# A list-scheduled hybrid decoder layer: two kinds of PSUM tiles change banks, and the schedule's transfer rate changes

## The chip, the cores and the metric

The kernel runs on one core of one Trainium2 chip. The metric is the device time of one execution in microseconds (us), taken as the median of several runs. Lower is better.

A core has a TensorE for matrix products (PE in the profile, with its weight loads as PEld), VectorE (DVE), ScalarE (ACT), GpSimd (POOL) and SyncE (SP). Here SP issues nearly all DMA transfers. TensorE writes its results to PSUM, which has eight banks; VectorE and ScalarE read them from there.

## The reference: what is computed

One layer over 4096 tokens of width 1024. The input is normalised, modulated with a scale and a shift from a conditioning vector, and projected once. The projection feeds three groups of heads in parallel:

- sliding-window attention (window 128, eight query heads, two key/value heads, with sinks and a distance penalty),
- RWKV-7 time mixing (four heads, a recurrent state with data-dependent decay and a delta rule),
- gated linear attention, GLA (four heads, in chunks).

```
h = rmsnorm(x, g_pre) * (1 + scale) + shift
proj = h @ w_in
attn = sliding_window_attention(q, k, v, sinks) * silu(ag)
rwkv = rwkv7_mixer(h, r, k, v, ...) * silu(rg)      # S = S*w + sa (kk*a) + v k ; y = S r
gla  = gla_mixer(h, q, k, v, ...) * silu(gg)
y = concat([attn, rwkv, gla]) @ w_out
out = x + gate * rmsnorm(y, g_post)
```

The change touches how two intermediate results of the RWKV part are held: the running sums of the log decay, from which the decay factors of a chunk come, and the transposed keys, which update the recurrent state.

## The kernel before

The tokens are cut into 16 steps of 256 (`NS`, `NT`). The kernel has two phases over these steps.

**First phase (about the first 1000 us).** For each step i a set of stages runs, each a Python generator:

- `stage_a` (line 1014) loads the tokens, normalises them and writes `hT`, the split f16 input of the projections; it uses PSUM tile `rb`.
- `stage_p` projects: tiles `pv`, `lp`, `zz` and `gqk`, all in bank pair `pj`. These are long runs of f16 products.
- `stage_d` (called "w") makes the gates and decays: `zp`, `gp`, `cgp`, then `wps` and `aps`, then the two tiles `cw`. A `cw` tile holds running sums of the log decay for one of the two 64-token chunks of each half step: a matmul of the decays `gw` with a constant triangular table. ScalarE reads each `cw` tile twice and writes `ep` and `em`, the exponentials of plus and minus the sums.
- `stage_qa`, `stage_qb` and `stage_qc` build and invert the triangular system inside a chunk: `np`, `atp`, then a pass through DRAM, then `Xp`, `Xq`, `Xp`, `X2`.
- `stage_k` (line 1470) transposes the keys: twice per step four 128x128 transposes go to a tile `kp`, and ScalarE copies it in three pieces to `BK`, of which there is one buffer.
- `stage_v` (`vp`, `bp`) and `stage_r` (`ktp`, `gap`, `kvp`, `op`, `ot`) do the values and the GLA part.
- `stage_q2` (line 1486) runs the recurrence over four chunks: `rp`, `up`, `sp`, `yp`, and at its end transposes the output in a tile `yt`.
- `stage_c` and `stage_g` convert the weights of the second phase on the side.

**Second phase.** `stage_s` does the projections for attention and the attention, `stage_m` mixes the three groups, and `outp` does the output projection with seven products per step (`op`), whose weights partly come in anew (`ov<-woscr`), and the last norm.

**PSUM.** The function `pst(tag, name)` (line 477) takes a 2 KB tile in the bank named by its tag. The tags are `pj` (two buffers), `m`, `mq`, `tr`, `at`, `sq` and `y`. With one buffer a tile can be written only when all reads of the tile before it under that tag are over, and tiles of a tag follow one another in the order in which the program asked for them. In the first phase `mq` serves `ktp`, one of the two `gap`, `kvp`, `ot`, `vp`, one of `np`, `bp` and `atp`, `Xp`, `Xq`, `X2`, `kp` and `yt`; `tr` serves `rb`, `aps` and one `cw`; `m` serves `zp`, `gp`, `cgp`, `wps` and the other `cw`; `at` serves `op` and the other `gap`, `np`, `bp` and `atp`.

**What sets the order.** Two planners act one after the other. `emit` (line 549) interleaves the stages: at each turn it takes the first stage, by rank, that can go on by a rough clock. A stage says with its `yield` what it waits for, tiles or bank names; `stage_k` names `mq` and `stage_d` names `m` and `tr`. So the order of the program comes about, and with it the order of tiles in each bank. Then `Order.pin` (line 222) makes a list schedule of every instruction of a phase: it keeps a ready time for each, takes the ready one with the lowest rank (its place in the program, with offsets for some), and fixes the order on each engine by dependencies. For a transfer it uses a table of landing times by size (3.5 us up to 512 KB, 4.8 us above) and a pipe shared by all transfers: a transfer lands no sooner than the pipe's time, which is at least 1.7 us after its issue and moves on by the bytes over a rate. `pin` is called for the first phase at line 1567 and for the second at line 2038. Transfers at the start of the second phase (its first weights) stand before that second list.

Of the kernel before, what the change touches and what calls it, by code (L numbers as in the profile page):

```python
# [33 lines left out]
LIFT = {}  # L34
LAG = {"l": 150}
URGENT = 150
TILING_WAIT = 0.6
LANES = ((0.06, 1.04e-3, VL), (0.02, 1.0e-3, AL), (0.1, 2.3e-3, 0.0), (0.0, 1e-3 / 2.4, PL), (0.05, 0.0, 2.0))

# [24 lines left out]
class Order:  # L64
# [157 lines left out]
    def pin(self):  # L222

        steps = self.steps
        ready = {e: {} for e in ENGINES}
        bursts, head = {}, list(range(len(steps)))
        for k, st in enumerate(steps):
            if st.eng == "PE":
                h = head[k - 1] if k else 0
                if k and steps[h].eng == "PE" and st.joint and st.joint == steps[h].joint and st.array[0] == steps[h].array[0]:  # L230
                    head[k] = h
                bursts.setdefault(head[k], []).append(k)
        left, when = [0] * len(steps), [0.0] * len(steps)
        for k, st in enumerate(steps):
            for j in [*st.needs, *st.turn]:
                if head[j] != head[k]:
                    left[head[k]] += 1
                    steps[j].then.append(k)
        for k, st in enumerate(steps):
            if head[k] == k and not left[k]:  # L240
                ready[st.eng][k] = 0.0
        free = dict.fromkeys(ENGINES, 0.0)
        cells, mode, table, pipe, half = [0.0] * 16, None, None, 0.0, {}
        last, count = {}, 0
        while count < len(steps):
            e = min((e for e in ENGINES if ready[e]), key=lambda e: max(free[e], min(ready[e].values())))
            now = max(free[e], min(ready[e].values())) + 1e-9
            at = sorted((k for k, t in ready[e].items() if t <= now), key=lambda k: (steps[k].rank, k))
            k = at[0]
            if e == "PE" and mode is not None and steps[k].array[0] != mode:  # L250

                same = [q for q in at if steps[q].array[0] == mode]
                wait = max(now - ready[e][q] for q in at if steps[q].array[0] != mode)
                if same and (mode != (4, 4) or wait < TILING_WAIT):
                    k = same[0]
            first = max(free[e], ready[e].pop(k))
            for k in bursts.get(k, [k]):
                st, t = steps[k], max(first, free[e])
                if e == "PE":
                    m, at, passes, took, issue = st.array  # L260
                    if mode is not None and m != mode:
                        t = max(t, max(cells)) + 0.094
                    mode = m
                    t = max(t, max(cells[c] for c in at))
                    for c in at:
                        cells[c] = t + passes * took
                    free[e], st.end = t + issue * passes, t + passes * took + 0.165
                else:
                    if st.half is not None:
                        was, half[e] = half.get(e, st.half), st.half  # L270
                        if was[0] != st.half[0] or None not in (was[1], st.half[1]) and was[1] != st.half[1]:
                            t = max(t, free[e] + 0.115)
                    if st.table is not None and st.table != table:
                        t, table = max(t, free[e] + 1.28), st.table
                    free[e], st.end = t + st.occ, t + st.lat
                    if st.bytes:

                        pipe = max(pipe, t + 1.7) + st.bytes / 310e3
                        st.end = max(st.end, pipe)
                st.start = t  # L280
                if e in last:
                    self.tc.add_manual_dep(
                        st.ins, last[e], mybir.DependencyInfo(mybir.DependencyClass.NoSync, mybir.DependencyReason.DATA))
                last[e], count = st.ins.name, count + 1
                for q in st.then:
                    to, h = steps[q], head[q]
                    left[h] -= 1
                    at = t if k in to.turn else 0.0
                    if k in to.needs and e != to.eng:
                        at = max(at, st.end + HOP_FROM[e] + HOP_INTO.get(to.eng, 0.0))  # L290
                    elif k in to.needs and (e == "SP" or e != "PE" and to.needs[k]):
                        at = max(at, st.end + (0.05 if e == "SP" else 0.03))
                    when[h] = max(when[h], at)
                    if not left[h]:
                        ready[to.eng][h] = when[h]
        self.forget()
# [104 lines left out]
def hybrid_kernel(ctx, tc, x, xc, rows, ada1, adaw, w1, wl, w2, wo, cst, abias, out):  # L401
# [8 lines left out]
    def pool_of(at, name, bufs=1, **kw):  # L410
        return model.order.pool(at.enter_context(tc.tile_pool(name=name, bufs=bufs, **kw)), bufs)
# [4 lines left out]
    st = pool_of(ctx, "small", 3)  # L416
# [57 lines left out]

    ps = pool_of(ctx, "ps", 1, space=PSUM)

    def pst(tag, name, bufs=1):
        bufs = 2 if tag == "pj" else bufs
        t = ps.tile([P, 512], F32, tag=tag, name=name, bufs=bufs)
        model.take(tag, bufs, t.tensor.name)  # L480
        return t
# [31 lines left out]
    def proj(po, W, c0, cw, hT):  # L513

        whi, wlo = W[0], W[1]
        n = 0
        for k in range(KD):
            for a, b in ((whi, 0), (whi, 1), (wlo, 0)):
                PE.matmul(po, a[:, k, c0 : c0 + cw], hT[:, b, k, :], start=(n == 0), stop=(n == 3 * KD - 1))
                n += 1  # L520
            yield
# [27 lines left out]
    def emit():  # L549

        while live:
            live.sort(key=lambda s: s[:2])
            best = None
            for s in live:
                if any(k[1] >= 0 and k not in done for k in s[4]):
                    continue
                t = max([s[5]] + [model.bank(b) for b in s[6]])
                if best is None or t < when:
                    best, when = s, t
                if t <= PE.clock:  # L560
                    break
            assert best is not None, [(s[2], s[1], s[4]) for s in live]
            PE.clock = max(PE.clock, when)
            model.now = PE.clock
            model.lift, model.stage, model.at = LIFT.get(best[2], 0), best[2], best[1]
            need = next(best[3], done)
            if need is done:
                done.add((best[2], best[1]))
                live.remove(best)
                continue  # L570
            need = () if need is None else need if isinstance(need, list) else [need]
            best[4] = [k for k in need if isinstance(k, tuple)]
            best[5] = max([PE.clock if not need else 0.0] + [model.time(t) for t in need if isinstance(t, bass.AP)])
            best[6] = [k for k in need if isinstance(k, str)]
# [65 lines left out]
    with ExitStack() as p1:  # L640
# [924 lines left out]
                    (8, "a", stage_a, i), (9, "c", stage_c, i), (10, "p", stage_p, i))  # L1565
        emit()
        model.order.pin()


    def pool2(name):  # L1570
# [78 lines left out]
    def heads_of(hT, q, kT, vt_, pj, pv):  # L1649
# [4 lines left out]
        yield from proj(kp[:, :NT], Wq[2], 0, P, hT)  # L1654
        model.order.urgent = URGENT
        for kv in range(2):
# [7 lines left out]
        for n in range(2):  # L1664
            yield ["pj"]
            qp = pj("qp")
            for b in range(2):
                yield from proj(qp[:, b * NT : (b + 1) * NT], Wq[n], b * P, P, hT)
            model.order.urgent = URGENT
            for kv in range(2):  # L1670
# [7 lines left out]
        for a in range(2):  # L1678
            yield from proj_tok(vp[:, a * P : (a + 1) * P], Wq[2], P, P, hT, a * P)
        model.order.urgent = URGENT  # L1680
        S.activation(vt_.rearrange("p a n -> p (a n)"), vp[:, :NT], AF.Identity, scale=Wq[2][2])
# [16 lines left out]
    def gates_of(hT, ag, pj):  # L1698

        for n in range(4):  # L1700
# [4 lines left out]
            av = ag[:, 2 * n : 2 * n + 2, :].rearrange("p b n -> p (b n)")  # L1705
            model.order.urgent = URGENT
            S.activation(av, gp_, AF.Tanh, scale=g_h[n])
# [182 lines left out]
    def outp(i):  # L1890
# [31 lines left out]
        def full(n):  # L1922
            yield ["pj"]
            po = pjt("op")
            yield from product(po, n)
            f["po"] = po

        def add(to, z):
            model.order.urgent = URGENT
            V.tensor_tensor(to, f["po"], z, op=ALU.add)  # L1930
            model.order.urgent = 0
# [9 lines left out]
        for y, n in first:  # L1941
            yield from full(n)
            model.order.urgent = URGENT
            S.copy(y, f["po"])
# [290 lines left out]
```

## Time and profile before

The median of three runs is 2021.44 us, from 2020.94 to 2027.34. The profiled execution took 2023.94 us; its span, from the first to the last instruction, is 2022.1 us.

| Engine | busy us | share of the span | instructions |
|---|---|---|---|
| TensorE | 1919.5 | 95% | 24899 |
| TensorE weight loads | 1483.7 | 73% | 24899 |
| VectorE | 1506.7 | 75% | 4246 |
| ScalarE | 1130.1 | 56% | 2609 |
| GpSimd | 311.3 | 15% | 485 |

The transfers move 258.77 MB, a mean of 128 GB/s. The mean granted clock of TensorE is 0.989.

How to read it: busy time is the union of an engine's instructions. Matmuls are pipelined, so their durations overlap, and a busy TensorE is not one at its peak. In the rows, `out<-in` names the tile written and the tiles read, with buffer numbers left out; `xN` counts instructions, and the bracket gives the idle time of the engine before the first one and what ended it. Nearly all instructions are recorded by one helper and therefore carry the same line, 336; tiles tell them apart. Some matmul records can be missing from a trace.

### The profile page before, as it was taken

What the parts mean: (1) busy time and instruction counts of PE and PEld (TensorE: products, weight loads), DVE (VectorE), ACT (ScalarE), POOL (GpSimd) and SP (SyncE); (2) the same over time, 40 slices, a digit from 0 to 9 for tenths busy, and PEclk for the clock granted to TensorE, in tenths of its full rate; (3) what the DMA queues carried; (4) which work ended last, traced back from release to release, by engine and by line L of the source; (5) the groups of instructions that cost most, each with busy time, mean ns of one, the idle gap of its engine ahead of it and who ended that gap; (6) DMA issues with size and microseconds to landing.
All of it is one profiled execution on the core that took longest, in us unless ns stands there. A gap on an engine that the chain in (4) does not pass through costs nothing.

```text
span 2022.1 us, 59931 instructions
## 1 busy us (share of the span) xinstructions
PE 1919.5 (95%) x24899; PEld 1483.7 (73%) x24899; DVE 1506.7 (75%) x4246; ACT 1130.1 (56%) x2609; POOL 311.3 (15%) x485
## 2 busy tenths in 40 slices
PE   5899999999999999999989999999999999999997
PEld 1677787777787777877767678877778777787683
DVE  5777877887778887776758876777767777676866
ACT  5878778765866765555434544444454444444443
POOL 0622213262221222221100000000000000000001
PEclk8899999999999999999999999999999999999998
DMA  9464535353424411124243433344333443334414
GB/s 373 150 208 148 164 114 160 118 150 110 131 76 147 151 37 60 61 76 141 93 152 125 154 106 117 117 139 139 97 108 116 149 129 112 110 108 141 128 36 168
DMA packets 154267, 258.77 MB, mean 128 GB/s; under 512 B 49026, under 2 KB 100738, under 8 KB 147716
## 3 DMA queue, kind: packets, MB, share of 16 engines
q1 hardware_dynamic: 153844, 254.34, 38.8%
q8 instruction: 198, 3.24, 0.6%
q14 instruction: 81, 0.66, 0.1%
q10 hardware_dynamic: 144, 0.52, 0.1%
HBM read 193.98 MB, written 60.82 MB: 126 GB/s over the span
## 4 chain that ended last, share of the span: by engine, by line
PE 54%; DVE 22%; ACT 9%; DMA 8%; issue 4%; SPq 2%; POOL 1%; DVEq 0%; ACTq 0%; POOLq 0%
PE gp L336 16%; PE op L336 12%; PE zz L336 4%; PE qp L336 3%; PE pv L336 2%; PE lp L336 2%; PE kp L336 2%; PE sc L336 2%; DVE pr L336 2%; PE ovp L336 2%; DVE q L336 2%; DVE mtp L336 2%; SPq L336 2%; DMA cs<-in_wo 1%; DVE tsc L336 1%
## 5 line engine op out<-in xcount | busy, mean ns | idle before, releaser
L336 PEld LDWEIGHTS <-mtp 128*128 128x128 f16 x1344 | 130.7, 98 | 146.0 <-issue 6.3
L336 PE MATMUL op<-o,mtp 128*128 128x512 f16 x768 | 172.9, 380 | 0.0
L336 ACT ACTIVATE pr<-pr,nm,lsc 128x256 f32<-128x256 f32 (+1 forms) x256 | 149.0, 584 | 11.5 <-DVE nm L336 11.4
L336 PE MATMUL op<-ov,mtp 128*128 128x512 f16 x576 | 144.0, 381 | 3.6 <-DMA ov<-woscr 3.5
L336 PEld LDWEIGHTS <-hT 128*128 128x128 f16 x1536 | 120.5, 100 | 24.5 <-issue 3.9
L336 ACT ACTIVATE mtp<-yv,oi 128x1024 f16<-128x1024 f32 x30 | 34.5, 1149 | 155.1 <-DVE yv L336 114.4
L336 DVE CUSTOM_DVE_ANT_0 pr<-sc,ab,kept 128x256 f32<-128x256 f32 (+1 forms) x256 | 108.4, 475 | 15.5 <-PE sc L336 15.2
L336 POOL TENSOR_TENSOR ry<-sy,expo 128x1 f32<-128x1 f32 x30 | 19.1, 638 | 588.3 <-DVE sy L336 588.3
L336 PE MATMUL pv<-gvh,hT 128*128 128x272 f16 x512 | 101.0, 290 | 5.6 <-ACT hT L336 2.6
L336 DVE TENSOR_TENSOR yv<-op,yv 128x512 f32<-128x512 f32 x105 | 70.3, 681 | 47.3 <-PE op L336 33.4
L336 DVE SCALAR_TENSOR_TENSOR ag<-ag,gp 128x512 f32<-128x512 f32 x64 | 43.4, 678 | 67.8 <-ACT ag L336 67.7
L336 PE MATMUL zz<-hT,rh 128*128 128x256 f16 x512 | 91.8, 277 | 1.7 <-DVE x L336 1.7
L336 PE MATMUL lp<-hT,Lh 128*128 128x256 f16 x512 | 91.3, 274 | 1.7 <-issue 1.6
L336 PE MATMUL zz<-hT,kh 128*128 128x256 f16 x512 | 91.9, 273 | 0.0
L336 ACT ACTIVATE ag<-gp,gh 128x512 f32<-128x512 f32 x64 | 43.9, 686 | 83.3 <-PE gp L336 83.3
L336 PE MATMUL qp<-hT,q1h 128*128 128x256 f16 x512 | 86.3, 273 | 3.7 <-DVE kT L336 3.7
L336 PE MATMUL zz<-hT,vh 128*128 128x256 f16 x512 | 89.4, 275 | 0.0
L336 PE MATMUL gqk<-hT,gqkh 128*128 128x256 f16 x512 | 87.5, 273 | 1.1 <-DVE zb L336 1.1
L336 PE MATMUL gp<-hT,q5h 128*128 128x256 f16 x512 | 86.3, 273 | 0.0
L336 PE MATMUL qp<-hT,q0h 128*128 128x256 f16 x512 | 85.4, 273 | 0.0
L336 PE MATMUL gp<-hT,q3h 128*128 128x256 f16 x512 | 85.3, 273 | 0.0
L336 PE MATMUL gp<-hT,q6h 128*128 128x256 f16 x512 | 85.2, 273 | 0.0
(442 smaller groups left out, 5858.5 us busy)
## 6 DMA issues: line engine op xcount, KB each, us to landing
ov<-woscr SPq DMA_DIRECT2D x96, 512.0 KB, 4.5
xh<-in_x SPq DMA_DIRECT2D x32, 512.0 KB, 4.2
xt<-in_xc SPq DMA_DIRECT2D x16, 1024.0 KB, 8.3
hscr<-hT SPq DMA_DIRECT2D x16, 1024.0 KB, 5.0
hT<-hscr SPq DMA_DIRECT2D x16, 1024.0 KB, 4.8
x<-in_x SPq DMA_DIRECT2D x30, 512.0 KB, 4.3
out<-yv SPq DMA_DIRECT2D x30, 512.0 KB, 3.0
cs<-in_w SPq DMA_DIRECT2D x56, 256.0 KB, 3.5
```

The lines of the kernel that those rows point to most:

```text
L336: r = f(*args, **kw)
```

## The change

Three edits:

1. A table `HOME` sends a tile of a given name and tag to another tag. `kp`, asked for under `mq`, goes to `tr`; the `cw` asked for under `m` goes to `at`. The other `cw` stays in `tr`.
2. `pst` looks there as long as `first_phase` holds an element; it is cleared behind the first phase's `pin`. No tile of the second phase is moved.
3. In the list schedule of both phases the pipe's rate goes from 310e3 to 400e3 bytes per microsecond (310 to 400 GB/s). The rate in the rough clock of `emit` stays 310.

The bank names in the stages' `yield`s are not edited: `stage_k` still asks for `mq` to be free, and `stage_d` for `m` and `tr`.

```diff
+HOME = {('kp', 'mq'): 'tr', ('cw', 'm'): 'at'}
...
-                        pipe = max(pipe, t + 1.7) + st.bytes / 310e3
+                        pipe = max(pipe, t + 1.7) + st.bytes / 400e3
...
+    first_phase = [True]
+
     def pst(tag, name, bufs=1):
+        tag = HOME.get((name, tag), tag) if first_phase else tag
         bufs = 2 if tag == "pj" else bufs
...
         emit()
         model.order.pin()
+        first_phase.clear()
```

## The prediction

> **What bounds the kernel now.** I read the engine totals first, then busy time by stretch, then TensorE's waits, then the order of work around the two tiles that move.
>
> ```profile
> PE 1919.5 (95%) x24899; PEld 1483.7 (73%) x24899; DVE 1506.7 (75%) x4246; ACT 1130.1 (56%) x2609; POOL 311.3 (15%) x485
> ```
> ```profile
> core 0: us, PE busy (x) PEld busy (x) DVE busy (x) ACT busy (x) POOL busy (x), PEclk, DMA share, GB/s
> 0.00:100.00 100.00, 67.49 (x482) 42.25 (x483) 63.78 (x202) 69.41 (x131) 35.90 (x59) 0.89 0.72 260
> 100.00:955.00 855.00, 823.34 (x13386) 664.72 (x13388) 671.12 (x2076) 589.89 (x1288) 228.84 (x360) 0.99 0.38 119
> 955.00:1020.00 65.00, 61.26 (x1037) 48.68 (x1022) 47.52 (x167) 25.56 (x63) 12.45 (x18) 1.00 0.32 113
> 1020.00:1980.00 960.00, 938.75 (x9901) 716.00 (x9900) 700.35 (x1764) 432.45 (x1105) 28.14 (x43) 1.00 0.37 121
> 1980.00:2022.10 42.10, 28.67 (x123) 12.09 (x121) 23.97 (x39) 12.74 (x23) 6.01 (x6) 0.86 0.49 164
> ```
>
> TensorE is the bound: it is busy 95% of the span. The change leaves its instructions as they are, so only its idle time, and to a lesser degree its changes of tiling, can move. The idle time by stretch is the width less the PE column: 32.5 us in the start (0 to 100), 855 − 823.3 = 31.7 us in the first phase, 3.7 us where the phases meet, 960 − 938.75 = 21.3 us in the second phase, 13.4 us in the tail. The moved tiles can reach the 31.7 and the 3.7; the new transfer rate can reach all of it, through the order alone.
>
> What ends TensorE's waits in the first phase (waits of 100 to 955 us: total, times, longest):
>
> ```profile
> PE yt L336 <- DVE ysb L336: 4.4, 4, 3.1
> PE rp L336 <- DVE Sst L336: 3.1, 4, 2.0
> PE atp L336 <- DVE RA L336: 3.0, 2, 2.7
> PE op L336 <- DVE qb L336: 2.1, 2, 1.4
> PE up L336 <- DVE rs L336: 2.1, 4, 1.0
> PE Xq L336 <- issue: 2.1, 2, 1.4
> PE ktp L336 <- DVE bon L336: 1.7, 3, 1.2
> PE ot L336 <- DVE osb L336: 1.3, 3, 0.7
> ```
>
> No group is large. Each is a link of a chain that came late at a moment when no projection was ready to fill in. The order is written out by the list schedule, so a late link stops everything behind it on TensorE.
>
> **Part 1: the keys' transposes leave bank mq for bank tr.** Here is one step of the first phase, first TensorE's rows, then ScalarE's, that read the same tiles:
>
> ```profile
> 196.11 0.63 PE L336 MATMUL yt<-first,ysb 128*128 128x128 f32 x4 [0.65 <-DVE ysb L336]
> ...
> 199.43 0.66 PE L336 MATMUL kp<-first,KB 128*128 128x128 f32 x4
> ...
> 201.89 0.60 PE L336 MATMUL kp<-first,KB 128*128 128x128 f32 x4
> ...
> 204.19 0.66 PE L336 MATMUL vp<-first,zb 128*128 128x128 f32 x4
> ...
> 206.77 0.66 PE L336 MATMUL ot<-first,osb 128*128 128x128 f32 x4
> ```
> ```profile
> 197.11 2.27 ACT L336 ACTIVATE ysb<-yt,lnx 64x256 f32<-64x256 f32 x4
> ...
> 200.63 1.12 ACT L336 COPY BK<-kp 128x256 f32<-128x256 f32 x3
> ...
> 203.01 1.13 ACT L336 COPY BK<-kp 128x256 f32<-128x256 f32 x3
> ...
> 205.22 1.50 ACT L336 COPY UV<-vp 64x256 f32<-64x256 f32 x4
> ```
>
> These tiles share mq, a bank with one buffer. The last read of yt ends at 197.11 + 2.27 = 199.38 and kp starts at 199.43; the first kp's copies end at 201.75 and the second starts at 201.89; that one's end at 204.14 and vp starts at 204.19. Three handovers within 0.05 to 0.14 us: it is the bank, not data, that paces them. Taken out, the two kp tiles shorten this queue by 204.14 − 199.43 = 4.7 us a step. The step lasts 57.3 us: yt's first and last start divided by 13 intervals of 14 steps.
>
> ```profile
> L336 PE MATMUL yt<-first,ysb x56: 272/273/446, 196.1 to 940.8; 128*128 128x128 f32 x56
> ```
>
> What it is worth has two terms. (a) TensorE's own waits before kp, over the whole run:
>
> ```profile
> PE kp L336 <- ACT BK L336: 1.3, 3, 0.7
> PE kp L336 <- ACT ysb L336: 0.6, 1, 0.6
> ```
>
> kp after kp's copies, and kp after yt's copies: the bank both times, 1.9 us. In tr the two kp of a step still follow one another, so the 1.3 may stay; bounds 0 to −1.9. I take −1.9, since kp may now start before yt and lie under other work. (b) The head start of up to 4.7 us for vp, ot, Xp, Xq, ktp and what hangs on them. The links that sit on mq are, from the waits above, yt 4.4, Xq 2.1, ktp 1.7 and ot 1.3: 9.5 us together. The others (rp, atp, up, op) stood on VectorE's queue and no bank helps them. Bounds: −9.5 if all go, 0 if TensorE meets as many late links in the new order. I take two thirds, −6.3, because some stall passes to the next link. For the remaining steps the head start buys nothing: TensorE was busy with projections throughout.
>
> The new bank has room. Busy time of the instructions on kp, on cw and on rb (tr's longest tenant), in this order; the columns are PE, PEld, then for kp DVE and ACT, for cw ACT, for rb DVE:
>
> ```profile
> 100.00:955.00 855.00, 17.14 (x112) 12.71 (x112) 0.00 (x0) 30.94 (x84) 0.99 0.38 119
> 100.00:955.00 855.00, 10.75 (x480) 9.32 (x480) 18.33 (x60) 0.99 0.38 119
> 100.00:955.00 855.00, 5.87 (x28) 3.35 (x28) 33.64 (x28) 0.99 0.38 119
> ```
>
> rb and half of cw hold tr for some 40 + 15 us of 855; kp adds 17 + 31 = 48. With aps it stays a bank mostly free.
>
> **Part 2: half of cw leaves m for at.** cw's tiles are read for 18.33 us in all, so one half is 9 us of reading and 5 of TensorE, 1 us a step. Bank m was free by then anyway, as cw's input gw is made from the tile that stood in m before, so nothing is removed. In at it may wait for a gap, op or atp tile, and its burst of 64 matmuls needs both banks. Under a covering projection this costs nothing; uncovered, about a gap tile's stay, from the op wait above 2.1 / 2 = 1.05 us, in at most one step of three: +5. Taken 0, bounds 0 to +5.
>
> **Part 3: 400 instead of 310 GB/s in the list schedule.** No transfer changes; only the times at which the schedule thinks they land. What the chip does with many transfers queued, in the start:
>
> ```profile
> 23.00:35.00 12.00, 9.47 (x36) 1.30 (x36) 1.11 (x3) 0.50 (x1) 0.08 (x1) 1.00 1.03 407
> ```
> ```profile
> 27.00 1.05 PE L336 MATMUL adp<-stg,scolb 128*32 128x512 f32 x4 [0.22 <-DMA stg<-in_ada]
> 28.29 1.05 PE L336 MATMUL adp<-stg,scolb 128*32 128x512 f32 x4 [0.24 <-DMA stg<-in_ada]
> ```
>
> A 512 KB piece lands every 1.29 us, and 407 GB/s flow: 310 was too slow there (1.69 us a piece), 400 is right (1.31). But these pieces all have to come before anything else can start, so the start's 32.5 us of idle stay: 0, bounds −2 to +2. Later the transfers are mostly alone:
>
> ```profile
> ov<-woscr SPq DMA_DIRECT2D x96, 512.0 KB, 4.5
> hT<-hscr SPq DMA_DIRECT2D x16, 1024.0 KB, 4.8
> ```
>
> For a lone 512 KB the schedule's table (3.5 us) rules at both rates (1.7 + 1.69 or 1.31). For 1 MB it goes from 1.7 + 3.38 = 5.08 to the table's 4.8, which is what the row measures. TensorE waits for these loads hardly at all, over the whole run:
>
> ```profile
> PE op L336 <- DMA ov<-woscr: 3.5, 2, 2.3
> PE pv L336 <- ACT hT L336: 2.6, 1, 2.6
> ```
>
> So 0 in the second phase, bounds −3 to +6 (a different order among 938 us of dense work; the ov waits doubled and some). The Trainium skill, "DMA: Bandwidth & Descriptors", section Bandwidth, says that the HBM side binds a core's HBM to SBUF transfers at about 358 GB/s. By that 400 would be too fast a model; the row of 407 GB/s speaks against it. Its consequence stands below as a rival.
>
> **Sum.** −1.9 − 6.3 + 0 + 0 = −8.2 us. The profiled execution took 2023.94 us (span 2022.1), 2.5 us above the median of 2021.44. So 2015.7 against its own time, and 2013.3 against the median.
>
> **Rivals.**
> - *The idle time was covered* (0 to −3 us, 2020). For: TensorE's idle is 3.7% of the first phase, no wait row exceeds 4.4 us, so the projections already hide most handovers. A new order can lose as much as it gains. Against: three handovers in a row on one bank.
> - *A larger gain* (−18 us, 2003.5). The whole chain of a step moves forward and half of the first phase's 31.7 us goes, plus some 2 us where the phases meet. For: the waits on VectorE (rp, up, atp) may follow an earlier start. Against: VectorE is busy 671 of 855 us and keeps its own order.
> - *Bank tr becomes the stall: slower.* kp's copies write BK, of which there is one, and the previous step's last read of it (sp) must be over. The schedule may place kp's transposes early; then tr stands full until BK is free, and rb, which the next step's projections hang on (rb, xt, hT, pv), waits behind it by tile order. It decides from the point where rb is delayed by more than the projections still left. Price: the pv wait above, 2.6 us, in six of 16 steps: +15.6, 2021.44 + 15.6 = 2037. For: rb's own tenancy is the longest on tr, and projections are what hides everything else. Against: tr is mostly free, and step i's kp comes late in its life.
> - *The 400 sends loads' users too early: slower.* An ov load is landed 4.5 us after issue where the table says 3.5. Queued behind others it is now modelled shorter still by 0.38 us. If each of 16 steps takes on half of the 1.0 us that the table falls short: +8, 2021.44 + 8 = 2029.4. For: the two waits of 3.5 us already there. Against: the loads' lead is several products long, and lone 512 KB loads are modelled as before. By the page's 358 a queued piece would take 1.46 us where the schedule says 1.31, an estimate, and this rival would be likelier.
> - *The change does little in the second half*, as no moved tile lives there: that is inside the first case and gets no time of its own.
>
> **How the numbers follow.** Forecast 2013.3, chance 0.45, own range 2006 to 2020; covered 0.25; larger gain 0.08; tr stalls 0.12; loads too early 0.10. A measurement of this kernel can tell about 0.3% from no change, 6 us: the bounds are 2015.4 and 2027.5. Forecast gives 0.30 faster and 0.15 same; covered 0.03, 0.20 and 0.02; larger gain 0.08 faster; tr stalls 0.01 same and 0.11 slower; loads too early 0.02 same and 0.08 slower. Together 0.41 faster, 0.38 same, 0.21 slower. The range for 8 in 10 goes from the larger gain to between the two slower cases: 2002 to 2034.
>
> **What would show it.** Right: kp starts well before yt's copies end, vp follows yt or starts up to 4.7 us earlier, the two kp waits are gone, and TensorE's busy time is the same with 100 to 955 us holding some 8 us less idle, the second phase's length within 3 us. Wrong: waits of rb or pv of over 1 us a step (tr), more than 8 us of TensorE waiting for ov (rate), or a first phase of the old length with other waits in the list. A second phase that moves by more than 5 us would mean that the rate, not the banks, sets the result.

## The result, and the profile after

The changed kernel takes 2010.23 us (median of seven runs, 2004.62 to 2014.73), the kernel before 2023.05 us (median of seven, 2020.32 to 2027.34). The ratio is 0.9932, with a 95% interval from 0.9918 to 0.9946: faster by 0.7%. The profiled execution took 2010.31 us and its span is 2008.2 us, 13.9 us below that of before.

The engine totals of the changed kernel:

```profile
PE 1915.3 (95%) x24899; PEld 1481.6 (74%) x24899; DVE 1498.6 (75%) x4246; ACT 1130.5 (56%) x2609; POOL 311.9 (16%) x485
```

The instructions are the same in number on every engine. To see where the time went I cut both traces at 86 us, a fixed time, and at the start of the first key projection of the second phase, which tells how long the first phase took. Some work of the first phase still lies behind this second mark. First the kernel before, then the changed one; the columns are width, PE, PEld, DVE, ACT, POOL, clock, DMA share and GB/s.

```profile
0.00:86.00 86.00, 57.11 (x404) 33.96 (x405) 51.63 (x179) 57.36 (x106) 26.73 (x49) 0.90 0.78 288
86.00:961.80 875.80, 839.18 (x13600) 677.65 (x13598) 687.15 (x2111) 604.31 (x1317) 239.57 (x374) 0.99 0.39 121
961.80:2022.10 1060.30, 1023.22 (x10899) 772.12 (x10898) 767.96 (x1958) 468.39 (x1187) 45.05 (x63) 0.99 0.37 121
```
```profile
0.00:86.00 86.00, 55.72 (x348) 31.83 (x352) 53.75 (x171) 56.14 (x104) 29.85 (x51) 0.88 0.80 290
86.00:948.80 862.80, 836.12 (x13638) 676.72 (x13639) 680.57 (x2124) 607.74 (x1322) 236.13 (x370) 1.00 0.39 122
948.80:2008.20 1059.40, 1023.50 (x10919) 773.02 (x10917) 764.23 (x1954) 466.64 (x1184) 45.91 (x65) 0.99 0.37 121
```

The first phase lost 13.0 of the 13.9 us. What follows took 1060.3 us and now takes 1059.4. Within the first phase TensorE's idle time went from 875.8 − 839.18 = 36.6 us to 862.8 − 836.12 = 26.7 us, and its busy time from 839.2 to 836.1.

What ends TensorE's waits in the first phase of the changed kernel (100 to 942 us):

```profile
PE yt L337 <- DVE ysb L337: 4.5, 4, 1.7
PE cgp L337 <- DVE gl L337: 2.3, 3, 1.2
PE vp L337 <- DVE zb L337: 2.2, 2, 1.6
PE vp L337 <- DVE AT L337: 2.0, 2, 1.5
PE Xq L337 <- DVE Xs L337: 1.7, 3, 0.8
PE ot L337 <- DVE osb L337: 1.6, 2, 1.1
...
PE ktp L337 <- DVE bon L337: 0.8, 2, 0.5
...
PE kp L337 <- ACT BK L337: 0.6, 1, 0.6
...
PE rp L337 <- DVE Sst L337: 0.5, 2, 0.3
...
PE op L337 <- ACT osb L337: 0.2, 1, 0.2
PE atp L337 <- DVE tc L337: 0.2, 1, 0.2
```

The links that I had named did not go away: yt, Xq, ktp and ot stood at 9.5 us and stand at 8.6. Other waits on VectorE did. rp for Sst went from 3.1 to 0.5; the rows of atp for RA (3.0) and of op for qb (2.1) are gone, and the largest rows left for these two tiles have 0.2 each. New are the two rows of vp, 4.2 us together: before, TensorE never waited for vp in this stretch.

One step in the middle, TensorE's rows of the kernel before and then of the changed one:

```profile
669.06 1.09 PE L336 MATMUL yt<-first,ysb 128*128 128x128 f32 x4 [3.14 <-DVE ysb L336]
...
673.62 0.60 PE L336 MATMUL kp<-first,KB 128*128 128x128 f32 x4
...
675.67 0.60 PE L336 MATMUL kp<-first,KB 128*128 128x128 f32 x4
...
680.12 0.75 PE L336 MATMUL Xp<-D,ATm 32*32 32x32 f32 x64
...
693.97 0.60 PE L336 MATMUL vp<-first,zb 128*128 128x128 f32 x4
...
701.99 1.31 PE L336 MATMUL atp<-RA,KB 64*64 64x128 f32 x32
```
```profile
660.03 0.38 PE L337 MATMUL kp<-first,KB 128*128 128x128 f32 x2
661.71 0.63 PE L337 MATMUL yt<-first,ysb 128*128 128x128 f32 x4 [1.30 <-DVE ysb L337]
662.17 0.38 PE L337 MATMUL kp<-first,KB 128*128 128x128 f32 x2
...
664.79 0.60 PE L337 MATMUL vp<-first,zb 128*128 128x128 f32 x4
...
665.91 0.61 PE L337 MATMUL kp<-first,KB 128*128 128x128 f32 x4
...
668.77 1.10 PE L337 MATMUL atp<-RA,KB 64*64 64x128 f32 x32
...
673.25 0.74 PE L337 MATMUL Xp<-D,ATm 32*32 32x32 f32 x64 [0.40 <-DVE D L337]
```

In the changed kernel the first two of the four transposes of kp run 1.7 us before yt; in the other kernel kp starts 4.6 us after yt. And atp, the start of the triangular system of the step after next, comes 7.1 us after yt instead of 32.9. This step is the one with the largest change, so I counted all of them in both traces. kp starts before yt in 8 of 15 steps, where before it started 3.0 to 7.4 us after it in every step. atp comes on average 11.7 us after yt (5.8 to 24.0) instead of 20.2 (9.5 to 32.9), and vp 15.8 instead of 20.8, each over 14 steps. That atp comes before Xp, as here, holds in neither kernel for every step.

### The profile page after: what moved, and what is told of

It reads as the page before. It is cut to its first block, busy times and chain, and to the rows that moved or that the text cites. A ratio compares the mean times of both kernels' runs of the same rounds, so it can differ in the third digit from the quotient of the medians.

```text
span 2008.2 us, 59922 instructions
## 1 busy us (share of the span) xinstructions
PE 1915.3 (95%) x24899; PEld 1481.6 (74%) x24899; DVE 1498.6 (75%) x4246; ACT 1130.5 (56%) x2609; POOL 311.9 (16%) x485
## 4 chain that ended last, share of the span: by engine, by line
PE 59%; DVE 19%; ACT 8%; DMA 7%; issue 3%; SPq 2%; POOL 1%; DVEq 0%; ACTq 0%; POOLq 0%
PE gp L337 16%; PE op L337 12%; PE zz L337 6%; PE qp L337 4%; PE lp L337 2%; PE pv L337 2%; PE kp L337 2%; PE sc L337 2%; DVE q L337 2%; PE ovp L337 2%; DVE mtp L337 2%; SPq L337 2%; DMA cs<-in_wo 2%; DVE pr L337 1%; DMA cs<-in_w 1%
## 5 line engine op out<-in xcount | busy, mean ns | idle before, releaser
L337 PE MATMUL gp<-hT,q4h 128*128 128x256 f16 x512 | 86.1, 273 | 0.0
```

The lines of the kernel that those rows point to most:

```text
L337: r = f(*args, **kw)
```

## The experiments

Three theories stood against each other. A: kp's leaving mq is the gain, the rate and cw are nothing. B: the rate is the gain. C: any new order of the first phase moves the time by some 10 to 15 us either way, and the change was a lucky draw. Each kernel was timed in five rounds beside the kernel before on the same chip, whose medians were 2022.2, 2022.8 and 2021.0 us in the three groups.

**The rate alone.**

```diff
-HOME = {('kp', 'mq'): 'tr', ('cw', 'm'): 'at'}
+HOME = {}
```

> Only the rate of 400 GB/s, no tile moved. Theory A (the keys' transposes leaving mq are the gain, the rate is nothing): within 4 us of before, first phase (first phase-two kp product) at 962 +- 4 us. Rival B (the rate is the gain): -8 to -14 us. Rival C (any reordering of the first phase moves the time by some 10 us either way, and the change was lucky): anywhere from -12 to +12 us, with the idle of TensorE in the first phase moving by as much.

2037.18 us, ratio 1.0068 (1.0053 to 1.0082): slower by 0.7%. The rate is a loss, and the whole of it lies in the first phase:

```profile
0.00:86.00 86.00, 57.74 (x391) 33.78 (x392) 54.07 (x180) 57.60 (x106) 31.84 (x54) 0.88 0.79 290
86.00:978.00 892.00, 844.51 (x13613) 680.22 (x13611) 688.22 (x2109) 604.21 (x1317) 230.43 (x369) 0.99 0.38 119
978.00:2038.00 1060.00, 1023.42 (x10899) 772.58 (x10899) 767.80 (x1958) 469.28 (x1187) 44.47 (x63) 1.00 0.37 121
```

875.8 us became 892.0 us, the rest 1060.3 became 1060.0. Theory A's "nothing" and rival B both fall.

**Both tiles moved, rate 310.**

```diff
-pipe = max(pipe, t + 1.7) + st.bytes / 400e3
+pipe = max(pipe, t + 1.7) + st.bytes / 310e3
```

> Both tiles moved, rate 310 as before. Theory A: -10 to -14 us, first phase some 11 us shorter. Rival B: within 4 us of before. Rival C: anywhere from -12 to +12 us, not the sum's complement to the run with the rate alone.

2001.81 us, ratio 0.9888 (0.9872 to 0.9905): faster by 1.1%. That is −20.4 us, where theory A expected −10 to −14. It is the fastest kernel of this study, faster than the changed one, whose ratio was 0.9932.

```profile
0.00:86.00 86.00, 58.55 (x368) 34.69 (x369) 49.93 (x171) 56.64 (x106) 22.49 (x47) 0.88 0.78 287
86.00:939.60 853.60, 831.99 (x13616) 676.34 (x13615) 684.15 (x2124) 607.26 (x1320) 238.48 (x374) 1.00 0.40 124
939.60:1999.90 1060.30, 1025.19 (x10919) 773.95 (x10917) 764.16 (x1954) 465.76 (x1184) 46.02 (x65) 0.99 0.38 121
```

**Only kp moved, rate 310.**

```diff
-HOME = {('kp', 'mq'): 'tr', ('cw', 'm'): 'at'}
+HOME = {('kp', 'mq'): 'tr'}
```

> Only kp to tr, rate 310. Theory A: -8 to -14 us, about what both tiles give together. Rival C: no relation to the run with both tiles, from -12 to +12 us.

2006.82 us, ratio 0.9929 (0.9914 to 0.9944): −15.4 us against 2022.22. As theory A expected from kp, but not "about what both tiles give": cw's move adds 2001.81 − 2006.82 = −5.0 us.

**Only half of cw moved, rate 310.**

```diff
-HOME = {('kp', 'mq'): 'tr', ('cw', 'm'): 'at'}
+HOME = {('cw', 'm'): 'at'}
```

> Only half of cw to at, rate 310. Theory A: within 4 us of before (bank m was free by then). Rival C: from -12 to +12 us, though this bank was never short.

2038.28 us, ratio 1.0086 (1.0072 to 1.01): slower by 0.9%. The same edit that gives 5 us with kp out of mq costs 16 us with kp in it. That is no sum of parts, and rival C, that each reordering is a draw, had to be tested next.

**Is kp's gain there in every order?** Three kernels complete pairs that differ by kp alone, and one more has a rate between, without kp's move.

```diff
# kp and rate 400
+HOME = {('kp', 'mq'): 'tr'}
...
# cw and rate 400
+HOME = {('cw', 'm'): 'at'}
...
# rate 350 alone
+HOME = {}
+pipe = max(pipe, t + 1.7) + st.bytes / 350e3
...
# kp and rate 350
+HOME = {('kp', 'mq'): 'tr'}
+pipe = max(pipe, t + 1.7) + st.bytes / 350e3
```

> kp to tr at rate 400, cw not moved; to be set against the run with the rate alone (+15 us). Theory A (kp leaving mq shortens the first phase whatever else the order does): at least 8 us below the rate alone, so at most +5 us over before. Rival C (each reordering is a draw of its own, some 15 us either way): no relation, from -15 to +20 us.

> Half of cw to at, rate 400, kp left in mq; to be set against the changed kernel (2010.2), which differs by kp alone. Theory A: at least 8 us above the changed kernel, some 2020 to 2040. Rival C: from 1995 to 2040, as likely below the changed kernel as above it.

> Only the rate, at 350. If a faster modelled pipe is worse by its optimism, this lies between 2022 (310) and 2037 (400), some +6 us. Rival C: no order in the rate, from -15 to +20 us.

> kp to tr at rate 350, cw not moved; to be set against the rate of 350 alone. Theory A: at least 8 us below it. Rival C: as likely above it as below.

They took 2013.26 us (0.9953, 0.9938 to 0.9967), 2054.94 us (1.0151, 1.0135 to 1.0168), 2038.42 us (1.0073, 1.0058 to 1.0089) and 2006.54 us (0.9907, 0.9892 to 0.9922). Two expectations were missed: the second kernel lies above the 2020 to 2040 us that theory A named, and 350 alone costs as much as 400 instead of lying between 310 and 400. The five pairs, as ratios to the kernel before, the changed kernel in the last row:

| rate, cw | kp in mq | kp in tr | difference |
|---|---|---|---|
| 310, cw in m | 1 (before) | 0.9929 | −0.7% |
| 310, cw in at | 1.0086 | 0.9888 | −2.0% |
| 350, cw in m | 1.0073 | 0.9907 | −1.7% |
| 400, cw in m | 1.0068 | 0.9953 | −1.2% |
| 400, cw in at | 1.0151 | 0.9932 | −2.2% |

kp's move gains in all five, from 0.7 to 2.2%. Under rival C each pair had an even chance, so that five of five would be one case in 32, were they independent. So a real gain is shown for orders such as these, and its size depends on the order that it meets. Read across, cw's move costs 0.8 to 0.9% with kp in mq and gains 0.2 to 0.4% with kp in tr. The rate of 400 costs 0.4% with both tiles moved, 0.2% with kp moved, 0.7% with neither. The two steps of 0.2% are not clear of the noise, as the intervals overlap.

The slowest kernel, cw in at at rate 400, shows how such a loss looks:

```profile
86.00:992.60 906.60, 849.82 (x13421) 681.54 (x13420) 676.97 (x2103) 603.62 (x1314) 226.76 (x365) 0.98 0.37 114
```
```profile
PE rp L337 <- DVE Sst L337: 4.7, 4, 2.1
PE Xp L337 <- DVE D L337: 4.1, 4, 1.1
PE kp L337 <- ACT ysb L337: 3.8, 2, 2.4
```

906.6 − 849.8 = 56.8 us of idle, twice that of the changed kernel, and no wait row holds a tenth of it. The third row is a kp standing behind the yt in bank mq.

**Which planner makes the gain.** kp goes to tr at rate 310, but the first planner keeps it in its books under mq.

```diff
+        asked = tag
         tag = HOME.get((name, tag), tag) if first_phase else tag
...
-        model.take(tag, bufs, t.tensor.name)
+        model.take(asked, bufs, t.tensor.name)
```

> kp to tr at rate 310, but the first planner still books it under mq, so that the program order is as before and only the list schedule knows of the free bank. If the gain (-15 us with kp alone) comes from the list schedule's freedom: -10 to -18 us. If it comes from the other program order that the first planner makes: within 4 us of before. If both halves are needed: between.

2014.44 us, ratio 0.9968 (0.9954 to 0.9982). Between: 0.3% against the 0.7% of kp's move with both planners told. The list schedule's freedom alone gives some half (−6.6 of −15.4 us). That the other program order gives the rest is a subtraction: the opposite kernel, with only the first planner told, was not run, and parts do not add up here.

**Is it that kp stands behind yt?** yt goes to tr, kp stays, rate 310.

```diff
+HOME = {('yt', 'mq'): 'tr'}
```

> yt goes to tr instead of kp, kp stays in mq, rate 310. If what matters is that kp need not stand behind yt in the same bank and mq gets some 45 us freer: -8 to -20 us, first phase shorter by as much. If kp itself has to leave (its two tiles ahead of atp, vp and the rest): within 5 us of before.

2025.65 us, ratio 1.002 (1.001 to 1.003). No gain in the whole. So taking yt out from before kp and freeing mq does not bring what kp's own leaving brings. It is not a clean test of either, as yt now takes time in tr. In the trace, that of the fastest of its runs (2021.08 us), the stretch from 86 us to the first key projection is 6.0 us shorter than before and the rest 2.9 us longer.

**Is it that kp holds KB?** KB gets a second buffer, all PSUM tiles stay where they were, rate 310. To make room, the gate weights' buffer `gaw` loses its second one.

```diff
-KB = wt([P, 2, 4, 2, HD], "KB", 1)
+KB = wt([P, 2, 4, 2, HD], "KB", 2)
...
-t = wt([P, 1024], "stg" + tag, 2 if tag in ("RA", "UV") else 1, tag=tag)
+t = wt([P, 1024], "stg" + tag, 2 if tag in ("RA", "UV", "KB") else 1, tag=tag)
...
-aw = wt([P, 4, P], "gaw", 2)
+aw = wt([P, 4, P], "gaw", 1)
```

> All tiles as before, rate 310, but KB (what kp transposes, rewritten in the next step) gets a second buffer; to make room one loading buffer of the gate weights (gaw, used in about 100 us of the first phase) is taken. If kp's late place costs because it holds KB and so the next step's chain: -8 us or more. If it costs because it holds the bank mq: within 4 us of before.

2033.49 us, ratio 1.0062 (1.0043 to 1.0082): slower. No gain from a second KB shows. The lost gaw buffer is not separated from it, so the loss is not explained, and that kp's place costs by holding KB is not excluded.

**Is a slower modelled rate safer?** Both tiles moved, rate 250.

```diff
+pipe = max(pipe, t + 1.7) + st.bytes / 250e3
```

> Both tiles moved, rate 250. If a schedule that thinks transfers slower is safer (400: 2010, 310: 2002): 1994 to 2002. If 310 happened to be the better draw: anything from 2000 to 2016.

2009.57 us, ratio 0.9951 (0.9933 to 0.9968). Slower than 310 (0.9888) and near 400 (0.9932). With both tiles moved, 310 is the best of three and both sides lose, so "optimism costs" is not the explanation. With kp in mq 350 and 400 lose the same 0.7%; with kp alone moved, 350 (0.9907) is not worse than 310 (0.9929).

## Why the prediction was right or wrong

The time of 2010.23 us lies in the forecast case (2013.3, own range 2006 to 2020) and in the range of 2002 to 2034. The net direction was right; the terms behind it were partly not.

- **What bounds the kernel: right.** TensorE's idle time in the first phase was where the gain came from, 9.9 of 13.9 us. That its busy time would stay the same was wrong by 3.1 us there; the last section shows why.
- **(a) kp's own waits, −1.9: about right.** Of the two rows 0.6 us is left, kp after kp's copies. Over the whole run kp's row for KB (2.0) is gone too, and one for zs (1.0) is new.
- **(b) the head start on mq, −6.3: mechanism half right, place wrong.** That kp was the tile to move off mq is shown by five pairs. vp's head start is there too, 5.0 us on average against "up to 4.7". But yt, Xq, ktp and ot, on which I put the gain, lost 0.9 us of their waits, and vp's own waits rose to 4.2; rp, atp and op, which I had given to VectorE's queue as beyond a bank's help, lost 7.3 (8.2 to 0.9). The step I quoted, with vp right behind kp, was not typical: in the later step shown above vp came 18 us after kp, and in nine of 14 steps 22 us or more after yt. I read a chain from one early step. With kp alone moved the gain was 15.4 us, nearly twice terms (a) and (b).
- **Part 2, cw, 0 with bounds 0 to +5: wrong.** The sign and the size depend on kp: −5.0 us with kp moved, +16 us without. That a burst which needs two banks gets its place from whatever else stands in them, I had seen, and priced at a gap tile's stay; the order of the whole step moved instead.
- **Part 3, the rate, 0: wrong.** It costs 8.4 us here (2010.23 against 2001.81, from two groups of runs) and 15 us alone. I had looked for its effect in the start and in the second phase, where it has next to none: the first yt starts at 196.1 us before and at 198.3 with the rate alone, and the rest kept its length. The step that failed is that the sum has no term for the rate in the first phase: that it acts "through the order alone" was read as nothing. I had called the later transfers mostly alone from two rows; a third of the same list, 1 MB of the first phase, lands in 8.3 us where the schedule's table for a lone transfer says 4.8 (the first row below), so there the pipe could count. Through which transfer the rate changes the order is not known. The rival of loads sent too early named the wrong place too: TensorE's waits for ov fell from 3.5 to 1.3 us. The Trainium skill's 358 GB/s ("DMA: Bandwidth & Descriptors", section Bandwidth) is by the same section the share of a core when both cores of a memory domain stream; the 407 GB/s of the prediction's row are those of one core alone. The figure decides nothing here: at 250, below it, the kernel was slower as well.

```profile
xt<-in_xc SPq DMA_DIRECT2D x16, 1024.0 KB, 8.3
```
```profile
PE op L337 <- DMA ov<-woscr: 1.3, 2, 0.8
```

- **Rivals.** A stalled bank tr did not show: in the list after no row of rb or pv tells of a wait of over 1 us a step. The larger gain (2003.5) is what the two tile moves give without the rate, 2001.8. "Covered" is out, with a gain clear of the noise.
- **The sum.** Measured in turn: kp −15.4, cw −5.0, rate +8.4, together −12.0; between the medians of the result −12.8. Forecast −8.2 + 0 + 0. That the total came within 4 us is partly luck: kp and cw gave 12.2 us more than forecast, and the rate took 8.4 of it back.

What stays open: by which link kp's leaving helps. With yt moved instead, or with a second KB at the price of a gaw buffer, there is no gain, and some half comes by the list schedule alone. atp's lead goes with the time, loosely: it comes on average 11.4 us after yt with both tiles moved at 310 (2001.8 us), 14.6 with kp alone moved (2006.8), 20.6 with the rate alone (2037.2) and 26.5 in the slowest kernel (2054.9). That this is the cause was not tested, and in the kernel whose first planner kept kp under mq atp stood at 19.7, with some half of the gain there. Nor is it known why 310 is better than 350 and 400 with kp in mq, and better than 250 and 400 with both tiles moved.

## What to carry to other kernels

Where a list schedule writes the order, a "harmless" constant of its model or a tile in another bank is a new order of the whole phase: here such edits moved the time by 0.2 to 1.5% without adding or removing an instruction. So take a change of several parts to pieces, and test the part you believe in under several orders; a sign that holds in five pairs is a finding, a single run is not. The parts that don't hold up, here the rate, can then be dropped, and the kernel without it was the fastest.

## What was not expected of the hardware

TensorE's busy time is not a constant of its instructions. In the first phase it was 832.0 us in the kernel with both tiles moved and rate 310, 836.1 in the changed one, 839.2 before, 844.5 with the rate alone and 849.8 in the slowest kernel, with 21.6, 26.7, 36.6, 47.5 and 56.8 us of idle beside it, for nearly the same stretch of work (13420 to 13640 recorded matmuls of the 24899). Busy rises with idle, by about half as much.

Most of this rise is the granted clock, of which I had read only the mean of 0.99. The traces show spells of 3.4, 6.8 or 10.2 us in which it is 0.5. Here is the step shown above in the kernel before: first 3.4 us with the stall for yt and the 3.4 us behind it (the columns are as above, the clock is the third from the end), then TensorE's products in the spell and after it.

```profile
665.20:668.60 3.40, 0.72 (x7) 0.44 (x4) 3.18 (x12) 0.81 (x2) 2.72 (x2) 1.00 0.45 143
668.60:672.00 3.40, 2.94 (x16) 2.02 (x20) 2.82 (x6) 1.78 (x4) 2.46 (x5) 0.50 0.50 139
```
```profile
670.39 0.66 PE L336 MATMUL pv<-gvh,hT 128*128 128x272 f16 x2
670.84 0.43 PE L336 MATMUL pv<-gvl,hT 128*128 128x272 f16 x1
...
672.69 0.40 PE L336 MATMUL pv<-gvh,hT 128*128 128x272 f16 x2
672.92 0.28 PE L336 MATMUL pv<-gvl,hT 128*128 128x272 f16 x1
```

Two products take 0.45 us in the spell (670.39 to 670.84) and 0.23 us after it. Each spell of this stretch, in all five kernels, follows 3.4 us in which TensorE was busy for 57% of the time or less. In the order of the list above, TensorE is busy inside such spells for 3.4, 3.4, 15.6, 17.1 and 27.3 us. If half of that is lost, an estimate from the rows above, the loss is 1.7, 1.7, 7.8, 8.5 and 13.7 us, and without it the busy times would lie between 830 and 836 us. What is left of their spread is not explained.

If these spells come of the stalls before them, as their place suggests, a stall can cost more than its own length, and no row of waits shows the rest. Of the first phase's 13.0 us some 6 may be this (7.8 less 1.7), beside the 9.9 us of idle time and with 3 us more of other busy time. It is arithmetic on the traces: no run changed the clock alone.
